# The last output block of a transformer layer, multiplied for 128 tokens at a time instead of 256

## The chip, the cores and the metric

The kernel runs on one core of a Trainium2 chip. A core has five engines that run their own queues of instructions: TensorE (PE in the profile, with its weight loads shown apart as PEld), VectorE (DVE), ScalarE (ACT), GpSimd (POOL) and SyncE (SP), and DMA queues that SP, ACT and POOL issue to. Matmul results go to PSUM, which is split into banks; here four banks go by the name psa and four by psb, each 128 partitions by 512 float32 columns. The metric is the device time of one execution in microseconds; the time shown is the median of three runs, and beside it stands one execution taken by the hardware profiler.

## The reference

One layer works on 1024 latent tokens of width 1024 and 256 context tokens: a SwiGLU feed-forward block, a mixing block (retention and gated linear attention), a second SwiGLU block, and a norm. All of it is float32. Only the end matters here:

```python
x = x + 0.5 * m_l[8][:, None, :] * swiglu(modulate(rms_norm(x, norm3_w[i]), m_l[6], m_l[7]),
                                            ffn2_w1[i], ffn2_w3[i], ffn2_w2[i])
...
return rms_norm(x, final_norm_w)

def rms_norm(x, w):
    xf = x.astype(jnp.float32)
    y = xf * lax.rsqrt(jnp.mean(xf * xf, axis=-1, keepdims=True) + EPS)
    return (y * w.astype(jnp.float32)).astype(x.dtype)
```

So the second block's output product is added into x, and then every token is divided by its root mean square over all 1024 features and multiplied by a weight per feature. A token's norm can be known only when all 1024 of its features are done.

## The kernel before

x is held transposed: features on the partitions, tokens along the free axis, as eight row blocks of 128 features (k = 0 to 7) for each of two groups of 512 tokens. A large product in float32 is made of three products of type fp32r: each operand is split into a high part and the rest (`split`, L449 to L451: ScalarE writes the high part, VectorE the rest), and `mm3` (L453 to L457) multiplies high by high, high by rest and rest by high. Each of the three is one matmul with its own weight load of 128 columns. A product of plain float32 shows in the profile as two matmul records with two weight loads.

The second feed-forward block's output product is cut by a fast matrix multiplication scheme into seven block products of depth 1408 (11 pairs of 128, `NP`). `back2` (L918) handles the last of them. It first runs the other six (`back6`), loads and splits all 11 weight pairs `ws` and input pairs `ts` of the last, and then multiplies them into the four psa banks A[0] to A[3], one per row block of 128 features, that is k = 4 to 7. Of the 512 columns (tokens) of each bank, the first 256 (h = 512 - TAIL) are done for all four row blocks first, then the other 256 for one row block after the other (m = 0 to 3): 33 matmuls each of width 256 (`mms`, L869). `add4` (L890, its VectorE instruction is L893) multiplies an accumulator by a gate and adds it into x, for a range of columns.

Three generators do the norm, and `back2` advances them with `next`: `final` (L1995) for the group of 512 tokens (n1) and for the first 256 tokens of the other group (n0), and `final_tok` (L1954) for the last 256 tokens, called the tail. `final` writes its output transposed, from SP's queue (L2009). `final_tok` turns its part to tokens on the partitions: a matmul of a 128 by 128 piece of x with a diagonal matrix of the norm weights (`wd`, L1961) gives the piece transposed and weighted in a psb bank; two banks hold the 1024 features of 128 tokens. The squares of the row blocks (L582) are added up in `naccl` (L583). A row block is taken as soon as its add is done: the generator stops after k = 4, 5 and 6. The last step takes k = 7: a matmul of the sum of squares with a column of ones (L1970) puts one number per token on the partitions, in one column of a psa bank for each of the two groups b of 128 tokens; then come the squares of k = 7 (L1976), its transposes, and another L1970 product that adds to that column. `root` (L596) makes the factor per token by a logarithm (L600) and an exponential (L603). VectorE scales the first 512 features of the 128 tokens (L1991) and ScalarE the others (L1988); SP issues the DMA of the one (L1992), ScalarE's queue that of the other (L1989), each of 256 KB.

The order of instructions on an engine comes from the code, and the framework's scheduler may move an instruction that is ready ahead of one that is not. The semaphores that it sets follow from which tiles are read and written.

Of the kernel before, what the change touches and what calls it, by code (L numbers as in the profile page):

```python
# [17 lines left out]
P = 128  # L18
# [4 lines left out]
NP = NF // 2  # L23
# [397 lines left out]
class Trunk:  # L421
# [496 lines left out]
    def back2(self):  # L918
        slots = [f"{tg}{k}" for tg in range(2) for k in range(KD)]
        A = self.back6()  # L920
        ws, ts = [], []
        for p in range(NP):
            with self.tc.high_priority(offset=WPRI):
                t = self.hslot(slots[4 + p])
                self.split(self.raw_half(self.gd[4, p]), *t)
                ts.append(t)
                w = self.hslot((slots[15:] + slots[:4])[p - 6]) if p >= 6 else tuple(self.tile(self.fp, [P, 512], F32R, "s", self.ns) for _ in "hl")
                self.split(self.w2_tile(4, p), *w)
                ws.append(w)
        h = 512 - TAIL  # L930
        n1, n0, tail = self.final(1, 0, 512, self.nf, (4, 5, 6, 7, 0, 1, 2, 3)), self.final(0, 0, h, self.nf, range(KD)), None
        for n in (n1, n0, n1):
            next(n)
        for p in range(NP):
            for m in range(4):
                self.mms(A[m], ws[p], ts[p], m, p, False, 0, h)
        self.add4(0, 1, A, 0, h)
        next(n1), next(n0)
        tail = self.final_tok(0, h, TAIL, self.nf)
        for m in range(4):  # L940
            for p in range(NP):
                self.mms(A[m], ws[p], ts[p], m, p, False, h)
            if m == 0:
                next(n1), next(n0)
            if m == 1:
                next(n0)
            if m == 3:
                next(tail)
            for o in range(h, 512, 512 - h if m < 3 else P):
                self.add4(0, 1, A, o, 512 if m < 3 else o + P, (m,))  # L950
            if m:
                next(tail)

    def t34_raw(self, k):
        F = lambda t: t.bitcast(F32)
# [82 lines left out]
    def turn(self, z, a, q, bank):  # L1038
        ps = bank()
        for m in range(4):  # L1040
            self.nc.tensor.transpose(ps[:, m * P:(m + 1) * P], z[:, m * P:(m + 1) * P], self.ident)
        for m in range(4):
            x = self.x[2][4 * q + m][:, a * P:(a + 1) * P]
            self.nc.vector.scalar_tensor_tensor(out=x, in0=ps[:, m * P:(m + 1) * P], scalar=self.gates_m[1][:, 4 * q + m:4 * q + m + 1],
                                                in1=x, op0=ALU.mult, op1=ALU.add)
# [908 lines left out]
    def final_tok(self, tg, o, n, pool):  # L1954
        nc = self.nc
        nb = n // P
        acc = None
        pts = [[self.psB() for _ in range(2)] for _ in range(nb)]
        xs = [t[:, o:o + n] for t in self.x[tg]]
        at = lambda k, b: pts[b][k // 4][:, k % 4 * P:(k % 4 + 1) * P]  # L1960
        turn = lambda k, b: nc.tensor.matmul(at(k, b), xs[k][:, b * P:(b + 1) * P], self.wd[k // 4][:, k % 4 * P:(k % 4 + 1) * P],  # L1961
                                             start=True, stop=True)
        for k in range(KD - 1):
            acc = self.squares(xs, n, pool, "l", (k,), acc)
            for b in range(nb):
                turn(k, b)
            if k >= 4:
                yield
        last, r, ps = self.tile(pool, [P, n], F32, "nsql", NQ), self.tile(pool, [P, 8], F32, "nr", 2), self.psA()
        mm = lambda b, t: nc.tensor.matmul(ps[:, b:b + 1], t[:, b * P:(b + 1) * P], self.ones[:, 0:1], start=t is acc and b == 0,  # L1970
                                           stop=t is last, skip_group_check=True)
        for b in range(nb):
            mm(b, acc)
        for b in range(nb):
            s = slice(b * P, (b + 1) * P)
            nc.scalar.activation(last[:, s], xs[KD - 1][:, s], AF.Square)  # L1976
            turn(KD - 1, b)
            mm(b, last)
        for b in range(nb):
            s = slice(b * P, (b + 1) * P)  # L1980
            x = self.root(r[:, b:b + 1], ps[:, b:b + 1])
            if b:
                self.tc.add_manual_dep(x.ins, y.ins.name, SCHED, reason="order")
            for i in range(2):
                t = self.tile(pool, [P, 512], F32, "no", 8)
                dst = self.outt[s, i * 512:(i + 1) * 512]
                if i:
                    y = nc.scalar.activation(t, pts[b][i], AF.Copy, scale=r[:, b:b + 1])  # L1988
                    nc.scalar.dma_start(dst, t)  # L1989
                else:  # L1990
                    nc.vector.tensor_scalar(out=t, in0=pts[b][i], scalar1=r[:, b:b + 1], scalar2=None, op0=ALU.mult)  # L1991
                    nc.sync.dma_start(dst, t)  # L1992
        yield

    def final(self, tg, o, n, pool, ks):  # L1995
        nc = self.nc
# [387 lines left out]
```

## Time and profile before

| | |
|---|---|
| median of three runs | 2052.82 us (2051.63 to 2052.85) |
| the profiled execution | 2051.93 us |
| its span, first to last instruction | 2050.1 us |
| its granted TensorE clock | 0.998 |
| PE busy | 2037.2 us, 99% of the span |
| last block's second half of columns, m = 3 | 33 matmuls from 2037.56 us |
| last add (L893) starts | 2041.80 us |
| last output DMA issue on SP ends | 2046.48 us |

Times in the trace are counted from the span's start. A row of the timeline gives the start, the duration, the engine and line, the operation, the tiles written and read, and the shape of the output; "xn" is a run of n equal instructions. In brackets stands how long the engine was idle before it, and what it waited for. A matmul's duration is longer than the distance to the next one, since matmuls are pipelined: for cost, the distances between starts are to be read.

### The profile page before, as it was taken

What the parts mean: (1) busy time and instruction counts of PE and PEld (TensorE: products, weight loads), DVE (VectorE), ACT (ScalarE), POOL (GpSimd) and SP (SyncE); (2) the same over time, 40 slices, a digit from 0 to 9 for tenths busy, and PEclk for the clock granted to TensorE, in tenths of its full rate; (3) what the DMA queues carried; (4) which work ended last, traced back from release to release, by engine and by line L of the source; (5) the groups of instructions that cost most, each with busy time, mean ns of one, the idle gap of its engine ahead of it and who ended that gap; (6) DMA issues with size and microseconds to landing.
All of it is one profiled execution on the core that took longest, in us unless ns stands there. A gap on an engine that the chain in (4) does not pass through costs nothing.

```text
span 2050.1 us, 33385 instructions
## 1 busy us (share of the span) xinstructions
PE 2037.2 (99%) x11969; PEld 1726.5 (84%) x11969; DVE 1520.2 (74%) x2754; ACT 998.7 (49%) x1836; POOL 59.5 (3%) x97
## 2 busy tenths in 40 slices
PE   9999999999999999999999999999999999999998
PEld 8998888888888888898888888888888888888888
DVE  5888789899876788855677468778766766765686
ACT  4865433433445446655565355455444343344554
POOL 0000000000000000001021001100000000010000
PEclk9999999999999999999999999999999999999999
DMA  9764565677788766665322233251344444577774
GB/s 357 247 193 167 173 204 199 216 247 242 245 299 303 256 235 192 215 185 144 91 87 92 89 112 93 82 186 67 128 134 164 158 141 159 165 235 232 223 234 150
DMA packets 210311, 376.37 MB, mean 184 GB/s; under 512 B 23904, under 2 KB 44128, under 8 KB 210016
## 3 DMA queue, kind: packets, MB, share of 16 engines
q1 hardware_dynamic: 209568, 373.57, 55.7%
q8 instruction: 94, 1.54, 0.3%
q14 instruction: 73, 0.60, 0.1%
q10 hardware_dynamic: 576, 0.66, 0.1%
HBM read 292.74 MB, written 73.01 MB: 178 GB/s over the span
## 4 chain that ended last, share of the span: by engine, by line
PE 94%; DVE 2%; DMA 2%; ACT 1%; issue 0%; POOL 0%; SPq 0%; ACTq 0%; DVEq 0%; POOLq 0%
PE psa L147 25%; PE psa L455 10%; PE psa L456 10%; PE psa L457 10%; PE psb L147 10%; PE psb L455 9%; PE psb L456 9%; PE psb L457 9%; DMA raw<-gd 1%; DMA hh<-in_w 1%; DMA raw<-in_w 0%; DVE x L893 0%; DMA cx<-in_ctxP 0%; DVE hl L147 0%; DVE nt L147 0%
## 5 line engine op out<-in xcount | busy, mean ns | idle before, releaser
L450 ACT ACTIVATE whi<-raw 128x512 fp32r<-128x512 f32 x385 | 243.1, 632 | 514.1 <-issue 180.3
L451 DVE TENSOR_TENSOR wlo<-raw,whi 128x512 fp32r<-128x512 f32 x385 | 264.8, 688 | 157.6 <-ACT whi L450 154.9
L455 PE MATMUL psa<-hh,whi 128*128 128x512 f32 x676 | 263.2, 389 | 0.9 <-ACT s L744 0.9
L457 PE MATMUL psa<-hh,wlo 128*128 128x512 f32 x676 | 263.0, 389 | 0.0
L456 PE MATMUL psa<-hl,whi 128*128 128x512 f32 x676 | 263.0, 389 | 0.0
L147 PE MATMUL psa<-hh,whi 128*128 128x512 f32 (+1 forms) x664 | 233.7, 353 | 1.4 <-ACT hh L147 1.2
L147 PE MATMUL psa<-hh,wlo 128*128 128x512 f32 (+1 forms) x664 | 232.9, 351 | 0.3 <-DVE wlo L147 0.3
L147 PE MATMUL psa<-hl,whi 128*128 128x512 f32 (+1 forms) x664 | 232.5, 351 | 0.0
L455 PE MATMUL psb<-hh,whi 128*128 128x512 f32 x584 | 227.5, 389 | 0.0
L456 PE MATMUL psb<-hl,whi 128*128 128x512 f32 x584 | 227.3, 389 | 0.0
L457 PE MATMUL psb<-hh,wlo 128*128 128x512 f32 x584 | 227.2, 389 | 0.0
L147 DVE TENSOR_TENSOR wlo<-raw,whi 128x512 fp32r<-128x512 f32 (+1 forms) x217 | 139.9, 663 | 76.9 <-ACT whi L147 75.0
L147 ACT ACTIVATE whi<-raw 128x512 fp32r<-128x512 f32 (+1 forms) x217 | 129.1, 608 | 123.2 <-PE psa L147 96.7
L455 PEld LDWEIGHTS psa<-hh,whi 128*128 128x128 f32 x676 | 126.9, 188 | 27.7 <-ACT s L744 1.4
L457 PEld LDWEIGHTS psa<-hh,wlo 128*128 128x128 f32 x676 | 126.9, 188 | 26.3
L456 PEld LDWEIGHTS psa<-hl,whi 128*128 128x128 f32 x676 | 126.9, 188 | 26.3
L147 PEld LDWEIGHTS psa<-hh,whi 128*128 128x128 f32 x664 | 126.1, 190 | 17.7 <-ACT hh L147 1.7
L147 PEld LDWEIGHTS psa<-hh,wlo 128*128 128x128 f32 x664 | 126.1, 190 | 16.1 <-issue 0.6
L147 PEld LDWEIGHTS psa<-hl,whi 128*128 128x128 f32 x664 | 126.0, 190 | 15.2 <-DVE hl L147 0.2
L456 PEld LDWEIGHTS psb<-hl,whi 128*128 128x128 f32 x584 | 109.6, 188 | 23.0 <-DVE hl L451 0.4
L457 PEld LDWEIGHTS psb<-hh,wlo 128*128 128x128 f32 x584 | 109.6, 188 | 22.8
L455 PEld LDWEIGHTS psb<-hh,whi 128*128 128x128 f32 x584 | 109.6, 188 | 22.6
(498 smaller groups left out, 4170.5 us busy)
## 6 DMA issues: line engine op xcount, KB each, us to landing
raw<-in_w SPq DMA_DIRECT2D x316, 256.0 KB, 3.4
gd<-s SPq DMA_DIRECT2D x154, 256.0 KB, 3.1
raw<-gd SPq DMA_DIRECT2D x102, 256.0 KB, 3.0
ada<-in_adaT SPq DMA_DIRECT2D x48, 512.0 KB, 4.1
s<-in_w SPq DMA_DIRECT2D x66, 256.0 KB, 4.6
hh<-in_w SPq DMA_DIRECT2D x55, 256.0 KB, 4.5
sd<-s SPq DMA_DIRECT2D x44, 256.0 KB, 2.9
raw<-sd SPq DMA_DIRECT2D x44, 256.0 KB, 3.3
```

The source lines that it names most:

```text
L147: self.rec.add(self.eng, lambda: f(*map(get, a), **{x: get(v) for x, v in k.items()}), outs, ins, name, a, k)
L450: nc.scalar.activation(hi, src, AF.Copy)
L451: (eng or nc.vector).tensor_tensor(out=lo, in0=src, in1=hi.bitcast(F32), op=ALU.subtract)
L455: mm(ps, wa[0], xa[0], start=start, stop=False, skip_group_check=more)
L456: mm(ps, wa[0], xa[1], start=False, stop=False, skip_group_check=more)
L457: return mm(ps, wa[1], xa[0], start=False, stop=stop, skip_group_check=more)
```

## The change

For the last row block (m = 3) the 256 tail columns are no longer multiplied in one go. The loop over the two ranges of 128 columns now encloses the products: first all 11 pairs for the tokens of group b = 0, then all 11 for those of b = 1. Between the two stands the step of `final_tok` for k = 6, which was behind both, and the add of the first range. In `final_tok` the last step is split by group: the root, scaling and DMA of b = 0 now follow directly on its row sum, and the generator stops after each group. `back2` calls the step for b = 0 while it multiplies the second range, after its seventh pair (p = 6), and the step for b = 1 behind the second add. For m = 0 to 2 the inner loop has one turn, and the order is the one before.

```diff
         for m in range(4):
-            for p in range(NP):
-                self.mms(A[m], ws[p], ts[p], m, p, False, h)
-            if m == 0:
-                next(n1), next(n0)
-            if m == 1:
-                next(n0)
-            if m == 3:
-                next(tail)
             for o in range(h, 512, 512 - h if m < 3 else P):
-                self.add4(0, 1, A, o, 512 if m < 3 else o + P, (m,))
-            if m:
-                next(tail)
+                e = 512 if m < 3 else o + P
+                for p in range(NP):
+                    self.mms(A[m], ws[p], ts[p], m, p, False, o, e)
+                    if o > h and p == NP // 2 + 1:
+                        next(tail)
+                if m == 0:
+                    next(n1), next(n0)
+                if m == 1:
+                    next(n0)
+                if m == 3 and o == h:
+                    next(tail)
+                self.add4(0, 1, A, o, e, (m,))
+                if m in (1, 2) or o > h:
+                    next(tail)
@@ final_tok
             turn(KD - 1, b)
             mm(b, last)
-        for b in range(nb):
-            s = slice(b * P, (b + 1) * P)
             x = self.root(r[:, b:b + 1], ps[:, b:b + 1])
@@
-        yield
+            yield
```

## The prediction

> **What bounds the kernel now.** I read the page's first part, then the granted clock, the chain of waits over the last 12 us, and last the timeline there instruction by instruction.
>
> ```profile
> PE 2037.2 (99%) x11969; PEld 1726.5 (84%) x11969; DVE 1520.2 (74%) x2754; ACT 998.7 (49%) x1836; POOL 59.5 (3%) x97
> core 0: 2050.1 us, clock 0.998
> ```
>
> TensorE (PE) is busy for 99% of the span at nearly full clock, so work added to it early would show at once. The edit sits in the last 13 us of a span of 2050.1 us. There the timeline reads (start, duration, engine, line, operation, shape, count):
>
> ```profile
> 2037.56 0.36 PE L455 MATMUL psa<-hh,s 128*128 128x256 f32 x1
> 2037.76 0.28 PE L456 MATMUL psa<-hl,s 128*128 128x256 f32 x1
> ...
> 2041.47 0.28 PE L457 MATMUL psa<-hh,hl 128*128 128x256 f32 x1
> 2041.48 0.54 PEld L1961 LDWEIGHTS psb<-wd,x 128*128 128x128 f32 x4
> 2041.60 0.61 PE L1961 MATMUL psb<-wd,x 128*128 128x128 f32 x4
> 2041.80 0.61 DVE L893 SCALAR_TENSOR_TENSOR x<-psa,mod,x 128x128 f32<-128x128 f32 x2 [3.01 <-PE psa L457]
> 2041.93 0.53 PEld L1970 LDWEIGHTS psa<-ones,naccl 128*128 128x128 f32 x4
> 2042.04 0.50 PE L1970 MATMUL psa<-ones,naccl 128*128 128x1 f32 x4
> 2042.18 0.57 ACT L1976 ACTIVATE nsql<-x 128x128 f32<-128x128 f32 x2 [3.85 <-DVE x L893]
> 2042.41 0.47 PE L1961 MATMUL psb<-wd,x 128*128 128x128 f32 x2
> 2042.71 0.28 PE L1970 MATMUL psa<-ones,nsql 128*128 128x1 f32 x2
> 2042.86 0.47 PE L1961 MATMUL psb<-wd,x 128*128 128x128 f32 x2
> 2043.16 0.28 PE L1970 MATMUL psa<-ones,nsql 128*128 128x1 f32 x2
> 2043.48 0.26 ACT L600 ACTIVATE nr<-psa,mhalf 128x1 f32<-128x1 f32 x1 [0.73 <-PE psa L1970]
> 2043.77 0.20 ACT L603 ACTIVATE nr<-nr 128x1 f32<-128x1 f32 x1
> 2044.01 0.69 ACT L1988 ACTIVATE no<-psb,nr 128x512 f32<-128x512 f32 x1
> 2044.01 0.75 DVE L1991 TENSOR_SCALAR no<-psb,nr 128x512 f32<-128x512 f32 x1 [1.60 <-ACT nr L603]
> 2044.72 0.37 ACTq L1989 DMA_DIRECT2D out_tail<-no  x1
> 2044.78 1.70 SPq L1992 DMA_DIRECT2D out_tail<-no  x2
> 2045.37 0.75 DVE L1991 TENSOR_SCALAR no<-psb,nr 128x512 f32<-128x512 f32 x1 [0.62 <-ACT nr L603]
> ```
>
> The reader is to see three stretches. From 2037.56 to 2041.60 PE multiplies the last block: 33 products (11 pairs of depth times three), 256 tokens wide. From 2041.60 to 2046.15 the tail runs in series: the transposes by a diagonal (L1961), the adds into x (L893), squares, row sums (L1970), logarithm and exponential (L600, L603), scaling, and two issues on each of two queues (SP's last starts at 2044.78 + 1.70 - 0.33 = 2046.15, an issue lasting 0.33). The rest, 3.95 us, is the last 512 KB landing and the program's end:
>
> ```profile
> L1992 SPq DMA_DIRECT2D out_tail<-no x2: 332/332/333, 2044.8 to 2046.2; - x2
> DMA to landing us min/median/max: 2.6/2.8/3.0
> ```
>
> So the end hangs on the chain last product, add, square, row sum, root, scaling, landing. Only its middle 4.55 us can be overlapped.
>
> **The change part by part.** The 33 products of the last block become 66 of half the width: 33 matmuls and 33 weight loads more. The adds, squares, roots, scalings and DMAs stay in number.
>
> *Price of a product 128 tokens wide.* The trace has no such fp32r product, so it is bounded. The 256-wide ones start every (2041.47 - 2037.76) / 31 = 0.1197 us. The 512-wide ones:
>
> ```profile
> 1999.64 0.39 PE L456 MATMUL psb<-hl,whi 128*128 128x512 f32 x1
> ...
> 2004.40 0.39 PE L456 MATMUL psb<-hl,whi 128*128 128x512 f32 x1
> ```
>
> These are 21 products apart, 0.2267 us each. The line through both widths, 0.42 ns per column and 0.0127 us besides, gives 0.066 us at 128: the lower bound. The upper bound is the F32 product of that very form, 128*128 128x128: each takes two records, and four records stand 0.45 us long on the chain of waits, so 0.224 us per product.
>
> ```profile
> 2041.76 0.45 PE psb L1961 x4
> L1970 PEld LDWEIGHTS psa<-ones,naccl 128*128 128x128 f32 x4 | 0.5, 192 | 0.0
> L456 PEld LDWEIGHTS psa<-hl,hh 128*128 128x128 f32 x40 | 7.7, 192 | 0.0
> L147 PEld LDWEIGHTS psb<-zq,zk 128*32 128x32 f32 x1280 | 14.0, 110 | 7.9 <-issue 5.5 <-DVE qk L147 0.4 <-ACT zk L147 0.4
> L1041 PEld LDWEIGHTS psb<-ident,s 128*128 128x128 f32 x12 | 1.5, 139 | 0.4
> ```
>
> Between these lies what I take. The row sums move a single column, yet their four weight loads stand (0.53 - 0.192) / 3 = 0.113 us apart, and the four of the F32 products, 128 columns, (0.54 - 0.192) / 3 = 0.116: the width of the product has no part in it, the load of 128 columns does. The fp32r load takes the same 192 ns as theirs; the 32-column load takes 110, which makes 82 / 96 = 0.85 ns a column, 0.109 us for 128. Only the transposes through ident load faster, 139 ns. At 256 columns the stream (0.1197) just hides the load; at 128 (0.066) it can't. I take 0.112 us, by the rows of the row sums, which it is nearest to, and between the ends: halving the width saves almost nothing per product.
>
> The Trainium skill, "TensorE: Matmul & The Clock Gate", section "LDWEIGHTS (loading the stationary operand)", gives a load P / 1.2 ns, 107 for 128 columns; its section "Back-to-back issue gap" gives about 81 ns for a sustained 128-wide pair, and by that the sum below would be +0.8 instead of +2.6 us. The rows of 0.113 speak for the first.
>
> *First half.* 33 x 0.112 = 3.70 us from 2037.56: 2041.26, its last product starting at 2041.15.
>
> *Transposes of the seventh row block*, moved between the halves: 0.45 us, until 2041.71. Before, they stood behind all products.
>
> *A wait that is new.* The add of the first half reads the accumulator that the second half writes. The row of L600 shows how such sharing is held: the first root waited until 2043.48, though its own sum had started at 2042.71 and ScalarE was free from 2042.75; it began only when the second column's sum in the same tile had ended. So I let the second half wait for the add: it starts 0.33 after the last product's start (2041.47 to 2041.80) and lasts 0.35, the row below. 2041.15 + 0.33 + 0.35 = 2041.83, the second half at 2041.85. The wait costs 0.14; the transposes hide the rest, and without them it would be 0.59. Behind it stand all 33 products and the row sums of PE's queue. Bounds: 0 to 0.59.
>
> ```profile
> L893 DVE SCALAR_TENSOR_TENSOR x<-psa,mod,x 128x128 f32<-128x128 f32 x2 | 0.6, 346 | 3.0 <-PE psa L457 3.0
> ```
>
> The Trainium skill, "PSUM — Partial Sum Buffer", section "PSUM bank collisions raise a hardware error", asks that PSUM be guarded by bank and not by address: this speaks against halving within one bank. By it the sum has the 0.14; without it 0.14 less.
>
> *Second half.* 21 products (p = 0 to 6), 2.35 us: 2044.20. Then the first half's tail work on PE, as long as before from 2042.04 to 2042.86: 0.82, until 2045.02. Twelve products, 1.34: 2046.36, the last starting at 2046.25.
>
> *What the cover must hide.* The first half's last row sum starts at 2044.20 + 0.67 = 2044.87 (before 2042.04 to 2042.71), its root 0.32 later, the scaling 0.53 after that at 2045.72. It holds VectorE until 2046.47, and ScalarE with its DMA issue (0.71 + 0.37) until 2046.80. Both stand in their queues ahead of the second half's add (wanted at 2046.58) and square (2046.96): margins of 0.11 and 0.16 us. So this work costs nothing, barely; without cover it costs up to the 0.75 of one scaling. On SP the first pair passes nothing: the other outputs were issued by 2037.53.
>
> ```profile
> 2037.13 0.40 SPq L2009 DMA_DIRECT2D out_xT<-no  x1
> ```
>
> *The end.* Add at 2046.25 + 0.33 = 2046.58. PE is idle by then, so the transpose starts at 2046.95 and takes 0.30; the square (0.38 after the add's start, 0.31 long) ends at 2047.27; row sum 2047.29; root 0.32 later, 2047.61; exponential 2047.90; scaling 2048.14; issue 0.77 later at 2048.91, against 2046.15: +2.76. Landing: the first pair is out of the way, so between nothing and 0.4 (3.0 to 2.6) is gained; I take 0.2.
>
> *Sum.* +2.56. Products and wait add 66 x 0.112 - 33 x 0.1224 (4.04 over 33) + 0.14 = 3.5; the overlap gives back 0.7 to 0.8, landing 0.2. On the profiled execution, 2051.93 us, that is 2054.5. That execution lies 0.89 below the median of the three runs, 2052.82, so I forecast 2055.4.
>
> **The rivals.**
>
> *Slower: a narrow fp32r product takes what the F32 product of its form takes*, 0.224 us on PE at the last block. For it: no fp32r product narrower than 256 columns stands in the trace to say otherwise, and the form 128*128 128x128 is the nearest in shape. Against it: that F32 pair is two loads, the fp32r product one. First half until 2044.95, second from 2045.43 to 2053.64, last issue 2056.08: +9.9 - 0.2, 2062.5. It decides from the point where the loss passes 4.1 us: each ns of price costs 0.064 us, so from about 0.136 us a product.
>
> *The load hides and the stream rules*, 0.066 us. For it: the line through the widths, and 139-ns loads exist. Against it: 0.113 in the row sums. Products would end at 2043.37, but then the first half's scaling holds VectorE until 2044.03; the last issue is at 2046.38, and the time 2052.9, no change. By the page's 81 ns it would be 2053.6.
>
> *It does not overlap*: the first half's tail work is put behind all 66 products. For it: the order on an engine is not the code's everywhere (the row sum of L591 stands among products that the code puts ahead of it). Against it: it is ready 1.5 us before its place. Then the second half ends at 2045.55 and the 4.11 us from 2042.04 to 2046.15 follow whole: +3.5, 2056.3.
>
> ```profile
> 2026.95 0.39 PE L591 MATMUL psb<-nhi,one 128*128 128x256 f32 x1 [0.79 <-ACT nhi L450]
> ```
>
> **How the numbers follow.** About 0.2%, 4.1 us, is what can be told from no change here. Forecast 0.60, of which 0.05 lands above 4.1 us; F32 rate 0.24, slower; stream or page 0.08, of which 0.02 faster; no overlap 0.08, of which 0.03 slower. So faster 0.02, same 0.66, slower 0.32. The likeliest case alone runs from 2054.2 to 2056.8 (the waits' bounds and the runs' 1.2 us). The range must reach the F32 rate to hold 8 in 10: 2053.2 to 2063.4.
>
> **What would show it.** The last block's L455 to L457 rows should be 66 of 128x128, starting every 0.112 us: 0.066 or 0.224 proves a rival. A gap of about 0.14 us should stand ahead of the second half, released by L893. The first out_tail pair should be issued at about 2046.5, before the last add, and the last about 2.6 us behind the last product. The prediction is wrong if the pitch lies outside 0.10 to 0.136, or if VectorE's add of the second half is released by L1991 rather than by the product.

## The result, and the profile after

The changed kernel takes 2055.85 us (median of 20 runs, 2052.90 to 2059.45), the kernel before 2052.68 us (20 runs, 2049.55 to 2056.73). The ratio is 1.0016 with a 95% interval of 1.0010 to 1.0022, that is 2 to 4.5 us slower. The loss is clear of the noise, but at 0.16% it is smaller than the 0.2% that was to be called a change (the interval's upper end lies just above it).

The profiled execution after the change took 2057.79 us. Its timeline over the last block, the same view as before the change (lines 1961 to 1976 of the kernel before stand 3 further down here, those from 1988 on 1 further down):

```profile
core 0 of [0], span 2056.0 us
2040.28 0.30 PE L455 MATMUL psa<-hh,s 128*128 128x128 f32 x1
2040.42 0.28 PE L456 MATMUL psa<-hl,s 128*128 128x128 f32 x1
...
2043.89 0.27 PE L457 MATMUL psa<-hh,hl 128*128 128x128 f32 x1
2044.00 0.66 PE L1964 MATMUL psb<-wd,x 128*128 128x128 f32 x4
2044.20 0.35 DVE L893 SCALAR_TENSOR_TENSOR x<-psa,mod,x 128x128 f32<-128x128 f32 x1 [2.69 <-PE psa L457]
2044.49 0.50 PE L1973 MATMUL psa<-ones,naccl 128*128 128x1 f32 x4
2044.86 0.31 PE L455 MATMUL psa<-hh,s 128*128 128x128 f32 x1
...
2047.24 0.43 PE L1964 MATMUL psb<-wd,x 128*128 128x128 f32 x2
...
2047.65 0.31 PE L455 MATMUL psa<-hh,hh 128*128 128x128 f32 x1
...
2048.36 0.75 DVE L1992 TENSOR_SCALAR no<-psb,nr 128x512 f32<-128x512 f32 x1 [3.81 <-ACT nr L603]
...
2048.91 0.27 PE L457 MATMUL psa<-hh,hl 128*128 128x128 f32 x1
2049.14 2.89 SPq L1993 DMA_DIRECT2D out_tail<-no  x2
2049.22 0.35 DVE L893 SCALAR_TENSOR_TENSOR x<-psa,mod,x 128x128 f32<-128x128 f32 x1
...
2050.92 0.75 DVE L1992 TENSOR_SCALAR no<-psb,nr 128x512 f32<-128x512 f32 x1 [1.34 <-ACT nr L603]
```

The first half's scaling does run beside the second half's products, as the change says (L1992 at 2048.36). Its transfers are issued just behind the last product (SP at 2049.14), ahead of the second half's add. But the last block now begins at 2040.28 and its last product starts at 2048.91: 8.63 us, where it was 3.91 (2037.56 to 2041.47). The second view, the landing of the output transfers:

```profile
L1993 SPq DMA_DIRECT2D out_tail<-no x2: 332/332/332, 2049.1 to 2051.7; - x2
DMA to landing us min/median/max: 2.7/2.9/3.3
```

A remark on how the kernels are compared. The start of the last block scatters between 2034.4 and 2040.5 us over the profiled executions of this study, whatever the kernel, and the whole time scatters with it. All edits lie behind that point. So beside the whole time I read two stretches that repeat to 0.02 us: from the first product of the last block to the start of the last output issue on SP, and from that product to the end of the span. Each row below is one profiled execution; the first three number columns and the span are in us from its start:

| kernel | first product | last product | last issue | span | to last issue | to the end |
|---|---|---|---|---|---|---|
| before | 2037.56 | 2041.47 | 2046.15 | 2050.14 | 8.59 | 12.59 |
| after | 2040.28 | 2048.91 | 2051.70 | 2056.02 | 11.42 | 15.74 |
| after, again | 2039.52 | 2048.15 | 2050.93 | 2055.25 | 11.42 | 15.74 |
| halves alone | 2040.45 | 2047.74 | 2052.46 | 2056.46 | 12.01 | 16.01 |
| halves alone, again | 2037.53 | 2044.82 | 2049.54 | 2053.54 | 12.01 | 16.00 |
| 192 and 64 columns | 2039.63 | 2046.89 | 2053.28 | 2057.29 | 13.65 | 17.66 |
| 64 and 192 columns | 2040.42 | 2047.74 | 2052.43 | 2056.44 | 12.01 | 16.02 |
| order alone | 2038.65 | 2042.57 | 2046.80 | 2050.80 | 8.15 | 12.15 |
| order alone, again | 2034.43 | 2038.35 | 2042.58 | 2046.59 | 8.15 | 12.16 |
| change with 33 products | 2038.05 | 2043.00 | 2045.93 | 2050.22 | 7.88 | 12.17 |
| change, first half's step late | 2036.62 | 2045.25 | 2048.92 | 2053.25 | 12.30 | 16.62 |
| order, issue moved to SP | 2039.93 | 2043.85 | 2047.86 | 2052.28 | 7.94 | 12.35 |
| one root for both groups | 2036.11 | 2040.03 | 2044.00 | 2048.96 | 7.89 | 12.86 |

By this the change costs 15.74 - 12.59 = 3.15 us, twice the same, in agreement with the 3.2 between the medians. For the kernel of the last row the column of SP's last issue says less than for the others, since ScalarE's queue issues its own last transfer behind it there (shown below).

### The profile page after: what moved, and what is told of

It is laid out like the page before. It is cut to its first block, busy times and chain, and to the rows that moved or that the text cites. A ratio compares the mean times of both kernels' runs of the same rounds, so it can differ in the third digit from the quotient of the medians.

```text
span 2056.0 us, 33450 instructions
## 1 busy us (share of the span) xinstructions
PE 2043.3 (99%) x12002; PEld 1731.7 (84%) x12002; DVE 1520.6 (74%) x2754; ACT 998.8 (49%) x1836; POOL 59.7 (3%) x97
## 4 chain that ended last, share of the span: by engine, by line
PE 91%; DMA 3%; DVE 3%; ACT 1%; issue 1%; POOL 0%; SPq 0%; DVEq 0%; ACTq 0%; POOLq 0%
PE psa L147 25%; PE psb L147 10%; PE psa L455 10%; PE psa L456 10%; PE psa L457 10%; PE psb L456 9%; PE psb L455 9%; PE psb L457 8%; DMA raw<-gd 1%; DMA raw<-in_w 1%; DMA hh<-in_w 1%; DVE hl L451 1%; DVE wlo L451 0%; PE psa L2040 0%; DMA hl<-in_w 0%
```

## The experiments

**The halves alone.** The products are cut in two, and everything of the tail stays behind them.

```diff
         for m in range(4):
-            for p in range(NP):
-                self.mms(A[m], ws[p], ts[p], m, p, False, h)
+            for o, e in ((h, h + P), (h + P, 512)) if m == 3 else ((h, 512),):
+                for p in range(NP):
+                    self.mms(A[m], ws[p], ts[p], m, p, False, o, e)
```

> The last block's products are halved as in the change (33 for the first 128 tokens, then 33 for the others), but the tail stays behind all of them, in the order of before. My theory (a narrow product costs its weight load, 0.112 us, and the overlap gives back some 0.5 to 0.7 us): from the first product to the last output issue on SP 8.59 - 4.04 + 66 x 0.112 = 11.94 us, against 8.59 before and 11.42 with the change; the time 3.3 us above before, ratio 1.0016. Rival (the overlap gives back nothing, the whole difference is the products): as with the change, 11.42.

Timeline of this kernel:

```profile
core 0 of [0], span 2056.5 us
2040.45 0.30 PE L455 MATMUL psa<-hh,s 128*128 128x128 f32 x1
...
2047.74 0.27 PE L457 MATMUL psa<-hh,hl 128*128 128x128 f32 x1
...
2051.09 1.70 SPq L1993 DMA_DIRECT2D out_tail<-no  x2
```

66 products take 7.29 us from first to last start, 0.112 each. The last issue starts at 2051.09 + 1.70 - 0.33 = 2052.46, the stretch is 12.01 (11.94 expected). So the price of the halves is 12.01 - 8.59 = 3.42 us, and the rest of the change gives back 12.01 - 11.42 = 0.59 up to the issue, and only 16.01 - 15.74 = 0.27 up to the end. From the last product to the last issue it is 1.93 us shorter with the change (2.79 against 4.72), but PE does part of that work among the products, which now take 1.34 longer from first to last start (8.63 against 7.29). That rest holds two things, the overlap and the order by group; the order alone, below, gains 0.44 on whole products, so the overlap by itself may be worth no more than 0.15. Halves with the order but without the overlap were not run. The whole time, 1.0035 of before (1.0021 to 1.0049), was twice what the stretch says; the last block had begun late in that program. Run once more beside the change:

> The halves without the overlap, once more: the first time the stretch to the last issue was 12.01 us (3.4 above before), but the whole time 6.9 us above before, and its last block had begun 2.9 us later in the profiled execution. Theory (the start of the last block scatters by some us from program to program and load to load, for reasons that lie ahead of the edit): the stretch is 12.0 again, and the time lies 2 to 7 us above before, 0.6 above the change on the trace's stretch. Rival (the narrow products cost something ahead of them): 6 to 8 us above before again, with the last block late again.

> The change itself once more, beside the run with the halves alone. Theory: from the first product of the last block to the last output issue on SP 11.42 us as before in this kernel, and the program's end 4.3 after that issue, since the last pair of transfers now runs by itself; the time 2.5 to 3.5 us above before. Rival (the 4.3 against 3.99 was chance): 4.0.

The halves alone gave 1.0012 (1.0003 to 1.0020) this time, the change 1.0015 (1.0006 to 1.0023), and both stretches repeated. By the medians the halves lay 2.3 us above before, the change 3.95, more than the 2.5 to 3.5 expected. The first 1.0035 was scatter ahead of the edit, which the intervals of one program's runs do not hold; it should not be read as a cost. What causes the scatter is not known.

**What sets the distance of narrow products.** The same with ranges of 192 and 64 columns: `((h, 448), (448, 512))`.

> As the first, but the last block is cut into 192 and 64 columns. Theory (the load of 128 weight columns sets the distance below 256): products start every 0.112 us at both widths, 3.70 us for each range of 33. Rival (a narrow fp32r product streams at two cycles a column, which would give 0.107 at 128 as well): about 0.160 us at 192 and 0.055 at 64. Rival (the stream alone, 0.42 ns a column and 0.0127 us): 0.093 and 0.040.

Timeline, second and last product of each range, and the busy time and granted clock in three windows:

```profile
2039.80 0.27 PE L456 MATMUL psa<-hl,s 128*128 128x192 f32 x1
...
2043.26 0.27 PE L457 MATMUL psa<-hh,hl 128*128 128x192 f32 x1
...
2043.43 0.28 PE L456 MATMUL psa<-hl,s 128*128 128x64 f32 x1
...
2046.89 0.31 PE L457 MATMUL psa<-hh,hl 128*128 128x64 f32 x1
...
2039.63:2043.37 3.74, 3.74 (x36) 3.74 (x35) 0.74 (x2) 0.42 (x1) 0.00 (x0) 1.00 0.22 73
2043.37:2046.90 3.53, 3.53 (x35) 3.53 (x33) 0.00 (x0) 0.00 (x0) 0.00 (x0) 1.00 0.00 0
2046.90:2050.40 3.50, 3.50 (x19) 3.50 (x18) 0.61 (x2) 0.57 (x2) 0.00 (x0) 0.51 0.00 0
```

At both widths 31 products lie (2043.26 - 2039.80) / 31 = (2046.89 - 2043.43) / 31 = 0.112 us apart, the same as at 128 and as between the row sums of one column. Neither two cycles a column nor the stream alone fits; what is constant is the load of 128 weight columns. That a matmul with its load costs 0.112 us whatever it loads is ruled out by a row of the kernel before, in which each load has 64 columns:

```profile
999.22 0.56 PE L147 MATMUL psb<-AB 64*64 64x64 f32 x12
```

Twelve starts 0.112 apart would take 1.23 us from first to last; here all twelve matmuls are done within 0.56. So the load of 128 columns is left as what sets the price. The third window shows something else: the column ahead of the last two is the granted clock, 0.51 for the tail's matmuls. The stretch came out at 13.65, 1.64 above the 12.01 of two equal halves, for products that cost the same: the tail's matmuls ran at half speed. With the narrow range first, `((h, 320), (320, 512))`:

> The last block cut into 64 and 192 columns, the narrow range first, the tail as before. With 192 and 64 the tail's matmuls ran at half clock from 2046.90 on, 3.5 us after the narrow products had begun. Theory (3.4 us of products that fill under a third of the array's time, 64 columns being 27 ns at full rate of a distance of 111, lower the granted clock): the clock falls about 3.4 to 6.8 us after the narrow range begins, inside the 192-wide range, whose products then start about every 0.187 to 0.222 us instead of 0.112. Rival (the clock fell because the block's end was near, as it does before the program's end): full clock through the 192-wide range and a fall, if any, in the tail.

```profile
2040.42:2044.11 3.69, 3.69 (x36) 3.69 (x35) 0.75 (x2) 0.42 (x1) 0.00 (x0) 1.00 0.23 76
2044.11:2047.86 3.75, 3.75 (x36) 3.75 (x35) 0.00 (x0) 0.00 (x0) 0.00 (x0) 1.00 0.00 0
2047.86:2050.00 2.14, 1.86 (x18) 1.77 (x16) 0.61 (x2) 0.81 (x3) 0.00 (x0) 1.00 0.00 0
```

The clock stayed at 1.00 throughout, and the stretch is the 12.01 of the equal halves. So the theory as I wrote it falls: 3.7 us of 64-wide products do not always lower the clock. The Trainium skill, "TensorE: Matmul & The Clock Gate", section "What's actually happening", has the clock follow the activity within a window of 3.4 us that runs freely. The trace's clock records agree as far as they go: in all 13 profiled executions the changes of the granted clock lie whole multiples of 3.413 us apart. In the first kernel the clock fell at 2046.99, so a window ran from 2043.58 to there, wholly within the narrow products (2043.37 to 2046.89 by their starts). In the second it fell only at 2052.31, which puts an edge at 2042.07, in the middle of the narrow products (2040.42 to 2044.11), so that no window held them alone. That fits both runs; but it is one fall in two runs, and what share of a window must be busy stays open. The kernels with 128-wide products kept the full clock through all of them.

**The order alone.** The products are whole, only the tail's last step is ordered by group, as in the change, and called twice after the last add.

```diff
             if m:
                 next(tail)
+            if m == 3:
+                next(tail)
@@ final_tok
-        for b in range(nb):
-            s = slice(b * P, (b + 1) * P)
             x = self.root(r[:, b:b + 1], ps[:, b:b + 1])
@@
-        yield
+            yield
```

> The other part alone: the products are whole as before (33, 256 wide), and only the last step of the tail is ordered by group, root and scaling of the first 128 tokens ahead of the row sum of the others in the code. Theory (an accumulator tile is held against a reader and a writer at once, whichever columns they use): the first root starts about 0.32 us after its own row sum's start, 0.45 earlier than before, and the second row sum waits until that root has ended; the last issue comes 0 to 0.2 us earlier or later than before, 8.4 to 8.8 us after the first product. Rival (no such hold, only queue order): the first root starts early, the second row sum does not wait. Second rival: the scheduler restores the old order, and the first root waits for the second row sum as before.

```profile
2038.65 0.36 PE L455 MATMUL psa<-hh,s 128*128 128x256 f32 x1
...
2043.81 0.28 PE L1972 MATMUL psa<-ones,nsql 128*128 128x1 f32 x2
2043.95 0.47 PE L1963 MATMUL psb<-wd,x 128*128 128x128 f32 x2
2044.12 0.26 ACT L600 ACTIVATE nr<-psa,mhalf 128x1 f32<-128x1 f32 x1 [0.28 <-PE psa L1972]
...
2044.44 0.30 PEld L1972 LDWEIGHTS psa<-ones,nsql 128*128 128x128 f32 x2 [0.21 <-ACT nr L600]
2044.44 0.38 PE L1972 MATMUL psa<-ones,nsql 128*128 128x1 f32 x2
...
2045.43 1.70 SPq L1992 DMA_DIRECT2D out_tail<-no  x2
```

The first root (L600) now starts 0.31 us after its own row sum. The second row sum starts 0.49 after the transposes ahead of it, where it was 0.30 before, 0.06 after the root has ended (2044.12 + 0.26); the weight load ahead of it waited for that root (in brackets). So the tile is held between reader and writer, whichever columns they use, as I had read it from L600 before the change. But the gain is larger than the 0 to 0.2 us expected: the whole chain behind the root moves ahead, 8.15 against 8.59. Timed:

> The order by group alone, timed. In the trace its stretch from the first product of the last block to the last output issue was 8.15 us, and to the program's end 12.15, against 8.59 and 12.59 before. Theory: 8.15 and 12.15 again; in whole time 0.4 below before, too little to be told (0.998 to 1.001). Rival (one look, by chance): 8.6 and 12.6.

The stretches repeat, 8.15 and 12.16. The ratio is 0.9998 (0.9989 to 1.0007): in whole time it can't be told from before.

**The change without its price.** 33 of the 66 narrow products are left out, so the sums of these features are incomplete:

```diff
-                for p in range(NP):
+                for p in range(0 if m < 3 else 5 if o == h else 6, NP):
```

> The change with half of the last block's products left out, so that 33 narrow ones remain: pairs 5 to 10 for the first 128 tokens, 6 to 10 for the others (these features come out short of part of their sum). It shows the overlap without its price. Theory: the stretch from the first product to the last output issue is that of the change less 33 x 0.112: 11.42 - 3.70 = 7.72 us, 0.9 below before, the whole kernel 0.9 us faster at most. Rival (the overlap's gain is bound by the products it runs under, and needs all of them): above 8.2 us.

```profile
2038.05 0.30 PE L455 MATMUL psa<-hh,s 128*128 128x128 f32 x1
...
2043.22 3.04 SPq L1993 DMA_DIRECT2D out_tail<-no  x2
```

The last issue starts at 2043.22 + 3.04 - 0.33 = 2045.93, a stretch of 7.88 against 7.72 expected; the overlap does not need all the products. Of the 0.16 beyond the expected, 0.15 lies between the last row sum and its root (0.57 us against 0.42 in the change): in this kernel the granted clock fell to half at 2044.14, during the row sum. To the end it is 12.17 us, 0.42 less than before, and 12.02 without that 0.15. The order alone gives 12.15, without any overlap. So even if narrow products cost nothing extra, running the halves beside each other would have brought little or nothing more than the order within the change.

**The cover taken away.** `p == NP // 2 + 1` becomes `p == NP - 2`.

> The change, with the first half's last step called after the tenth pair (p = 9) of the second half instead of the seventh: nine products later. It takes the cover away. Theory: the products end as before, but the first half's scaling on VectorE then runs until about 1.0 us later and the second half's add stands behind it: the add comes some 0.9 later, released by the scaling, and the stretch is 12.3 instead of 11.42. Rival (the scaling does not stand in the add's way): 11.4.

```profile
2045.25 0.28 PE L457 MATMUL psa<-hh,hl 128*128 128x128 f32 x1
...
2045.70 0.75 DVE L1992 TENSOR_SCALAR no<-psb,nr 128x512 f32<-128x512 f32 x1 [4.81 <-ACT nr L603]
2046.37 0.34 DVE L893 SCALAR_TENSOR_TENSOR x<-psa,mod,x 128x128 f32<-128x128 f32 x1
```

The last product starts at 2045.25, so the add was due 0.31 later, at 2045.56. VectorE was busy with the other half's scaling and began it at 2046.37, 0.81 late. The stretch grew from 11.42 to 12.30, as expected. With the step at the seventh pair the scaling ended just ahead of the add (0.11 us, see below); at the tenth it did not. No place between them was run.

**Two tries at the tail of the kernel before.** First, the order alone with the first group's second transfer issued from SP (`(nc.scalar if b else nc.sync).dma_start(dst, t)`):

> The products whole as before; the last step ordered by group as in the run with the order alone, whose stretch was 8.15 against 8.59; and the first group's second transfer issued by SP instead of ScalarE's queue. Theory (the chain runs through ScalarE: root, scaling, issue, second exponential, scaling): without the issue of 0.37 in its queue the second exponential follows its logarithm at once, 0.25 earlier: a stretch of 7.9, 0.7 below before, which the whole time (scatter of some us) cannot tell. Rival (the issues on SP, one behind the other, hold the end): 8.15 or more.

The issue came at 7.94, as expected, but the end at 12.35, later than the 12.15 of the order alone: now 4.41 us pass from the last issue to the end, against 4.00. Its ratio is 0.9996 (0.9987 to 1.0005). Second, one logarithm and one exponential on two columns, `self.root(r[:, :nb], ps[:, :nb])`, ahead of the loop over the groups:

> The products whole and the order as before, but one logarithm and one exponential for both groups (two columns at once) instead of two each. Theory (from the first issue on the DMA engines bound the end: 1 MB was written without a pause in 3.0 us): the last issue comes 0.6 earlier, a stretch of 8.0, but the program's end only 0.1 to 0.2 earlier, 12.4 to 12.5 after the first product. Rival (the second group's chain on ScalarE bounds the end): 12.0.

```profile
L1987 ACTq DMA_DIRECT2D out_tail<-no x2: 351/358/366, 2043.3 to 2044.4; - x2
L1990 SPq DMA_DIRECT2D out_tail<-no x2: 332/332/333, 2043.3 to 2044.0; - x2
DMA to landing us min/median/max: 2.7/3.2/3.6
```

SP's last issue is early, 7.89, ScalarE's at 2044.41 or 8.30 (8.53 before), and the end late, 12.86 against 12.59 before. My expectation that the end gains a little was wrong. Up to 3.6 us pass from issue to landing in this kernel, against 3.0 at most before. In both tries an earlier issue of the second pair did not bring an earlier end. The trace records each landing in 16 steps, and tells where the time went: counted from the first product, fifteen steps of the last transfer were there 0.1 us earlier than in the kernel compared with (10.80 against 10.91 with the order alone, 11.28 against 11.38 before), but the sixteenth came 0.6 us behind them, where it was 0.27 and 0.24.

## Why the prediction was right

The forecast was 2055.4 us by a loss of 2.56 in the profiled tail, called no change with a lean to slower; measured were 2055.85 and 3.15.

- *Price of a narrow product*: taken as 0.112, measured (2043.89 - 2040.42) / 31 = 0.112 in the change, and at 64 and 192 columns too. This step carried the forecast, and it was right for the reason given: the load of 128 columns sets the distance. The bounds 0.066 and 0.224, and the two rivals built on them, fall. The Trainium skill's 107 ns for such a load ("TensorE: Matmul & The Clock Gate", "LDWEIGHTS (loading the stationary operand)") is close to the measured 112 from start to start; its 81 ns for a sustained narrow pair (section "Back-to-back issue gap") is not what these products show.
- *The wait between the halves*: I had 0.14, with a gap released by L893 as its sign. That sign did not appear; PE has no gap there. The scheduler put the row sums of the first seven blocks (L1973 at 2044.49) into it, which I had placed behind the seventh pair. Between the halves lie 0.86 us instead of 0.59, in the middle of the second half 0.41 instead of 0.82: 1.27 in all against 1.41. The hold itself exists on the tile of the row sums, as the order alone showed; on the accumulator no run shows a wait, since the row sums last beyond the add (it ended at 2044.20 + 0.35 = 2044.55).
- *Cover*: the first half's scaling was to be off VectorE 0.11 us ahead of the second half's add. It ended at 2048.36 + 0.75 = 2049.11, the add began at 2049.22. The late variant showed the price of losing it, 0.88.
- *From the last product to the last issue*: 2.66 forecast, 51.70 - 48.91 = 2.79 measured.
- *What the overlap gives back*: 0.7 to 0.8 by my sum, 0.59 by the halves alone, of which the order by group may be up to 0.44. My sum did not tell the two apart. The rival without overlap falls, since L1992 runs among the products; but its 3.5 was not far from the truth in size.
- *Landing*: this is the term that was wrong, in size and in sign. I took 0.2 us of gain for the last pair alone on the DMA engines. From the last issue to the end it is 2056.02 - 2051.70 = 4.32, against 3.99 before: 0.33 lost. All four executions in which the first pair goes out well ahead show 4.29 to 4.32, and the seven in which both pairs go out as before 3.99 to 4.02. Before, the first pair did stand in the second's way at its start: SP's second transfer was issued at 2046.15, the first one's last packet ended at 2047.14, and the second's packets began 1.17 us after their issue, against 0.97 with the change. But by itself the pair took longer to write, and SP's last packet ended 2.42 us after the issue instead of 2.44: nothing gained. The loss lies behind the packets. Fifteen of the sixteen steps of the last landing came 2.84 us after the issue (2.78 before), the last step another 0.50 later (0.24 before). It is not for being alone: the first pair with the change was as much by itself, and SP's half landed 2.80 us after its issue with no late step. In all 13 traces the step is late (0.08 to 0.73 us) in just those output transfers of the tail that are still in flight when one 8 KB packet of the instruction queue runs, and not in the others (0.02 at most). The DMA view after the change, from 2043 us on, shows that packet (queue, packets, MB, share of the 16 engines):

```profile
q14 instruction: 1, 0.01, 0.1%
```

No experiment moved that packet, so why the last step comes later in some kernels stays open. With the 0.2 that did not come, the landing makes 0.53 of the 0.59 us by which the forecast loss fell short. Without the landing term the sum is 2.76, and the issue moved by 11.42 - 8.59 = 2.83.

That the median came within 0.45 us of the forecast owes something to luck: the halves alone lay 6.9 us above before in one program and 2.3 in the next, and the loss in the tail was 0.59 above the forecast.

## What to carry to other kernels

Before cutting a product to overlap its end, look for the width below which the weight load sets the distance: in this trace the load of 128 columns costs 0.112 us, and products of 192 and of 64 columns cost the same; one of 256 columns costs 0.120, so every product much narrower than that is paid for at nearly the full price. Halving 33 such products cost 3.4 us to win 0.3 to 0.6. And test the reordering without the cutting: a reader and a writer on one PSUM tile waited for each other, and emitting the first root ahead of the second row sum won 0.43 us of the tail, by the trace, with no product touched.

## What the runs showed of the hardware

The distance between products with a full weight load did not move from 0.112 us at widths of 64, 128 and 192 columns. In one of two kernels with 64-wide products the granted clock fell to half right behind them, which cost 1.64 us in the tail. The landing of the last output transfer ended with one late step of sixteen, 0.24 to 0.61 us behind the fifteenth, and in two kernels what an earlier issue had gained was lost to it.
